# Turning attention probabilities by DMA instead of on TensorE, in a two-layer decoder trunk

## The chip, the cores and the metric

The kernel runs on one core of one Trainium2 chip. Its metric is the device time of one execution in microseconds (us). The core's engines work in parallel, each through its own queue in order, and wait for each other by semaphores: TensorE (PE) multiplies matrices, VectorE (DVE), ScalarE (ACT) and GpSimd (POOL) do elementwise work, SyncE (SP) issues the DMAs. In the profile PEld is PE's weight load.

## The reference, cut to what matters

A sequence of 256 tokens of width 1024 goes through two layers, each an attention mixer and a SwiGLU feed-forward block (FFN), and a last normalisation, all in float32.

```python
def dilated_mixer(h, w_in, w_out):            # layer 0, "mixer A": 16 heads of 64
    proj = (h @ w_in).reshape(B, S, N_GROUPS, 3, N_HEADS, HEAD_DIM)
    for g, (window, dil) in enumerate(((128, 1), (512, 4), (2048, 16))):
        q, k = partial_rotary(proj[:, :, g, 0], pos), partial_rotary(proj[:, :, g, 1], pos)
        o, lse = dilated_band_attention(q, k, proj[:, :, g, 2], dil, window // dil)
    wts = softmax(stack(lses))                # the three patterns are mixed by their denominators
    return einsum('gbsh,gbshd->bshd', wts, stack(outs)).reshape(B, S, ATTN_WIDTH) @ w_out

def forgetting_mixer(h, w_in, b_f, w_out):    # layer 1, "mixer B"
    s = einsum('bihd,bjhd->bhij', q, k) * scale + c[i] - c[j]   # c: running sum of log forget gates
    return einsum('bhij,bjhd->bihd', softmax(where(j <= i, s, NEG_INF)), v) @ w_out

for i in range(2):
    h = h + mixer[i](rmsnorm(h, norm[i]))
    h = h + (silu(gate) * up) @ w_down        # FFN on rmsnorm(h)
return rmsnorm(h, final_norm)
```

Scores come out with queries on partitions. To multiply the probabilities p with the values, PE needs the keys on partitions, so every 128x128 block of p has to be transposed in between.

## The kernel before, in words

**Matmuls.** Every float32 operand of a projection is split into a high and a low part, and `mm3` (L200 to L209) issues three matmuls for each product: high by high (L203), and the two mixed ones (L208). Weights come in pieces of 512 KB over SP's queue (L101, five buffers); ACT makes the high part (L80), DVE the low part (L84). The list `order` names the weights in the order of use; loads run two units ahead. Results are split in the same way: the attention output `ot` has a high part `oth` from ACT and a low part `otl` from DVE.

**Mixer A** works in four quarters (hq) of four heads, two head pairs (pr) each. The list `a_units` sets the units: per quarter six query and key units (w 0 and 1 of the three patterns g) and its value units (w 2). A unit is 48 matmuls of 256 columns; units that are written as a pair, like the dilated values of a quarter (patterns 1 and 2) or the undilated ones of quarters 0 and 1, are projected together, by `proj_pair`, 512 columns wide. The undilated values of quarters 2 and 3 are units by themselves (`proj_tok`). POOL copies the dilated values into place, 16 small copies a quarter (L285).

**Steps of attention** (`scores_0`, `scores_12`, `softmax_a`, the transposes, `pv_a`, the product with the values) are put between units: `later(i, step)` puts one behind unit i. Quarters 0 to 2 transpose by DMA (`turn_a`): POOL copies p so that the 16-bit halves of its numbers lie apart (L528), SP issues a DMA transpose of 10 blocks for each head (L530), ACT puts the halves together again (L531). Quarter 3 and all of mixer B transpose on PE, by multiplying with the identity into PSUM (`transposed`, L301), from where ACT or DVE copies (L306).

**out_proj** multiplies `ot` with the output weights: for each half t of the tokens 16 items of three 512-column matmuls, one for each n (half of the width) and k (128 rows of the weights; rows 2 hq and 2 hq + 1 belong to quarter hq). Attention steps that are still due are put between the items of the first half; the norm of that half's result (`norm_t`) lies between the last items of the second.

**Mixer B** has the same build in `b_units`: each quarter has a query, a key and a value unit. `scores_b` ends in a softmax on DVE (L906, L916) and ACT (L908, L915), with a bias that POOL masks (L880). In the program before, the transposes (`trans_b`) come one and a half units after the scores' unit and the product (`pv_b`, L313) two units after it, for all four quarters.

**What sets the order.** The scheduler keeps one queue per engine. It places instructions by the estimated time at which they can start; those under `first()` are put ahead of others. Once built, each engine's order is fixed.

## Time and profile before

| | us |
|---|---|
| median of 3 runs | 736.87 (736.38 to 737.0) |
| the profiled execution | 736.1 |
| its span, first to last instruction | 734.3 |
| PE busy | 726.4 |
| DVE, ACT, POOL busy | 495.9, 388.7, 83.0 |
| mean granted PE clock | 0.997 |

A row of groups has line, engine, operation, output <- inputs, size and count, then busy time, mean duration in ns, and the engine's idle time before it with its main releaser. A row of the timeline has start and duration in us first. A row of one line's view has minimum, median and maximum duration in ns, then the first and the last start.

### The profile page before, as it was taken

How to read it: one execution, taken by the hardware profiler on the slowest of the kernel's cores; microseconds unless marked ns; L12 is line 12 of the kernel's file. 1: busy time of each engine (PE TensorE's matmuls, PEld its weight loads, DVE VectorE, ACT ScalarE, POOL GpSimd, SP SyncE). 2: the span in 40 equal slices, each digit the busy share in tenths (PEclk: the TensorE clock that was granted, in tenths of full speed). 3: DMA queues.
4: the chain of work that ended last, by engine and by line, in shares of the span. 5: the costliest groups of instructions: out<-in, count | busy, mean ns of one | idle time of the engine just before them, and what ended most of it. 6: DMA issues, size and time to landing. Idle time of an engine off the chain costs nothing.

```text
span 734.3 us, 14310 instructions
## 1 busy us (share of the span) xinstructions
PE 726.4 (99%) x5856; PEld 672.4 (92%) x5856; DVE 495.9 (68%) x762; ACT 388.7 (53%) x617; POOL 83.0 (11%) x118
## 2 busy tenths in 40 slices
PE   9999999999999999999999999999999999999996
PEld 7999989999988899999999989999889999999995
DVE  6997998998996775554555474576776554556533
ACT  7646747738445663444554453587475444545421
POOL 0600206007105000000000004110010000000001
PEclk9999999999999999999999999999999999999998
DMA  9865955956864376656567352874547656656601
GB/s 335 306 202 174 237 182 153 289 193 152 268 194 160 116 241 221 195 179 203 195 202 247 127 168 90 294 260 138 172 142 237 222 179 203 195 188 218 198 1 58
DMA packets 55042, 141.93 MB, mean 193 GB/s; under 512 B 20257, under 2 KB 21441, under 8 KB 54977
## 3 DMA queue, kind: packets, MB, share of 16 engines
q1 hardware_dynamic: 54832, 140.88, 59.4%
q8 instruction: 46, 0.75, 0.4%
q14 instruction: 20, 0.16, 0.1%
q10 hardware_dynamic: 144, 0.15, 0.1%
HBM read 136.00 MB, written 1.07 MB: 187 GB/s over the span
## 4 chain that ended last, share of the span: by engine, by line
PE 97%; DVE 1%; ACT 1%; POOL 0%; issue 0%; POOLq 0%; DVEq 0%; ACTq 0%
PE ps_mm L208 34%; PE ps_mm L203 17%; PE ps_tr L208 9%; PE ps_sc L208 8%; PE ps_o L208 7%; PE ps_tr L203 5%; PE ps_sc L203 4%; PE ps_o L203 4%; PE ps_o L313 2%; PE ps_sc L395 2%; PE ps_tr L196 1%; PE ps_tr L301 1%; PE ps_sc L476 1%; PE ps_o L322 1%; PE ps_sc L894 0%; PE ps_sc L458 0%
## 5 line engine op out<-in xcount | busy, mean ns | idle before, releaser
L80 ACT ACTIVATE wh<-raw 128x1024 fp32r<-128x1024 f32 x236 | 243.4, 1054 | 207.1 <-PE ps_tr L208 66.7
L84 DVE TENSOR_TENSOR wl<-raw,wh 128x1024 fp32r<-128x1024 f32 x236 | 288.3, 1242 | 82.6 <-ACT wh L80 82.4
L203 PE MATMUL ps_mm<-xt,wh 128*128 128x256 f32 x816 | 227.2, 279 | 0.2 <-ACT v L281 0.2
L208 PE MATMUL ps_mm<-xt,wl 128*128 128x256 f32 x816 | 226.0, 277 | 0.0
L208 PE MATMUL ps_mm<-xt,wh 128*128 128x256 f32 x816 | 226.0, 277 | 0.0
L203 PEld LDWEIGHTS ps_mm<-xt,wh 128*128 128x128 f32 x816 | 153.1, 188 | 2.2 <-issue 1.7
L208 PEld LDWEIGHTS ps_mm<-xt,wl 128*128 128x128 f32 x816 | 153.6, 188 | 0.1
L208 PEld LDWEIGHTS ps_mm<-xt,wh 128*128 128x128 f32 x816 | 153.4, 188 | 0.0
L208 PE MATMUL ps_tr<-xt,wh 128*128 128x256 f32 x304 | 83.9, 276 | 0.0
L208 PE MATMUL ps_tr<-xt,wl 128*128 128x256 f32 x304 | 83.9, 276 | 0.0
L203 PE MATMUL ps_tr<-xt,wh 128*128 128x256 f32 x304 | 83.7, 276 | 0.0
L730 DVE TENSOR_TENSOR sa<-ps_tr,sa 128x256 f32<-128x256 f32 x38 | 16.1, 424 | 73.5 <-PE ps_tr L208 73.5
L208 PEld LDWEIGHTS ps_tr<-xt,wh 128*128 128x128 f32 x304 | 57.1, 188 | 0.0
L208 PEld LDWEIGHTS ps_tr<-xt,wl 128*128 128x128 f32 x304 | 57.0, 188 | 0.0
L203 PEld LDWEIGHTS ps_tr<-xt,wh 128*128 128x128 f32 x304 | 57.0, 188 | 0.0
L203 PE MATMUL ps_mm<-wh,xt 128*128 128x512 f32 (+1 forms) x144 | 49.8, 346 | 0.0
L173 POOL TENSOR_SCALAR rs<-ssq 128x1 f32<-128x1 f32 x7 | 1.9, 271 | 420.6 <-ACT junk L182 420.6
L208 PE MATMUL ps_mm<-wl,xt 128*128 128x512 f32 (+1 forms) x149 | 49.1, 335 | 0.0
L208 PE MATMUL ps_mm<-wh,xt 128*128 128x512 f32 (+1 forms) x149 | 49.1, 335 | 0.0
L285 POOL COPY v<-v 32x256 f32<-32x256 f32 x64 | 40.5, 632 | 71.2 <-ACT v L281 68.6
L203 PE MATMUL ps_sc<-wh,ah 128*128 128x512 f32 x80 | 31.4, 392 | 0.0
L208 PE MATMUL ps_sc<-wl,ah 128*128 128x512 f32 (+1 forms) x82 | 31.3, 385 | 0.0
(232 smaller groups left out, 1113.6 us busy)
## 6 DMA issues: line engine op xcount, KB each, us to landing
raw<-in_gu SPq DMA_DIRECT2D x88, 512.0 KB, 4.8
raw<-in_a_in SPq DMA_DIRECT2D x68, 512.0 KB, 5.0
raw<-in_dn SPq DMA_DIRECT2D x44, 512.0 KB, 4.7
raw<-in_b_in SPq DMA_DIRECT2D x24, 512.0 KB, 5.0
raw<-in_a_out SPq DMA_DIRECT2D x8, 512.0 KB, 5.0
raw<-in_b_out SPq DMA_DIRECT2D x8, 512.0 KB, 4.4
bias<-sums SPq DMA_DIRECT2D x8, 384.0 KB, 6.6
grow<-in_norms SPq DMA_DIRECT2D x4, 512.0 KB, 5.7
```

The source lines that it names most:

```text
L80: a = nc.scalar.activation(view(hi), src, AF.Copy)
L84: return nc.vector.tensor_tensor(view(lo), src, view(hi).bitcast(F32), op=ALU.subtract)
L196: nc.tensor.transpose(tr[:, k * P:(k + 1) * P], xn[:, kk * P:(kk + 1) * P], ident)
L203: nc.tensor.matmul(o, sh, mh, start=start, stop=False)
L208: last = nc.tensor.matmul(o[:, u], s, m[:, u], start=False, stop=end and u.stop == n)
L285: nc.gpsimd.tensor_copy(v[1 + a % 2][n:n + 32, a // 2 * S:a // 2 * S + S], by_t[a * 32:a * 32 + 32, t, g])
L301: nc.tensor.transpose(tr[:, i * P:(i + 1) * P], b, ident)
L313: nc.tensor.matmul(o[h * HD:(h + 1) * HD], v[:, c:c + HD], w(h), start=start, stop=stop)
L322: nc.tensor.matmul(o[:, :n], mhalf.to_broadcast([P, P]), mhalf.to_broadcast([P, n]), start=True, stop=True)
L395: nc.tensor.matmul(lead[t], xt[y][:, k, t * P:(t + 1) * P], w[z][:, u], start=k + y + z == 0, stop=k == KT - 1 and z == 1)
L476: nc.tensor.matmul(sc[h][c, o:o + 64], q[HR[h], pr, qb * P + a * 32:qb * P + a * 32 + 32], k[HR[h], pr].rearrange("p (b n) -> p b n", b=2) ...
L730: nc.vector.tensor_tensor(a, u, sg, op=ALU.mult)
```

## The change

Every probability block of both mixers is now transposed by DMA. `transposed`, `trans_a` and `trans_b` are gone. In mixer A quarter 3 turns through rooms of its own (`apart0`, `apart1`, and two tiles for what comes back) that serve both head pairs in turn, and the result is written over p. In mixer B `turn_b` does it for a pair of heads at once: the first pair's halves are put apart by POOL, the second's by DVE, one transpose of 12 blocks follows, and ACT puts the halves together in two copies.

The undilated values of quarters 2 and 3 become one pair, the last unit of mixer A; so pv_a of quarters 2 and 3 move into out_proj, which is rewritten: with `at=(4, 16)` they stand before item 4 and item 16, where four items of the second token half have been moved ahead. The norm lies over 8 items of the second half instead of 12. In mixer B, pv_b of quarters 0 and 1 keep their places (behind units 7 and 9), that of quarters 2 and 3 go into out_proj, and quarter 3's scores come half a unit earlier.

```diff
-        a_units += (..., v12, [(hq, 0, 2)] + v12, v12 + [(hq, 0, 2)])[hq]
+        a_units += (..., v12, v12, v12 + [(2, 0, 2), (3, 0, 2)])[hq]
...
     def turn_a(quad, pr):
...
+        last = quad["hq"] == 3
+        if last and pr == 0:
+            quad["room"] = [(hrow(f"apart{h}")[:, :640], p_tile(640)) for h in range(2)]
         for h in range(2):
...
+            with first():
+                apart, turned = quad["room"][h] if last else (home(("pt", "bias")[pr]), None)
+                w = p if last else apart
+                apart = apart.bitcast(U16)
+                nc.gpsimd.tensor_copy(apart.rearrange("p (t c) -> p t c", t=2), parted(p))
+                if not last:
+                    turned = home(("bias", "pt")[pr * (h == 0)])
+                turned = turned.bitcast(U16)
+                nc.sync.dma_start_transpose(turned.rearrange("p (g c) -> p g c", c=P), apart)
+                nc.scalar.copy(parted(w), turned.rearrange("p (t c) -> p t c", t=2))
...
                     for pr in range(2):
-                        if hq == 3:
-                            later(step(hq) + pr, trans_a, quad, pr)
-                        else:
-                            later(j + 1, turn_a, quad, pr)
+                        later(j + 1, turn_a, quad, pr)
                     for pr in range(2):
-                        later(step(hq) + 2, pv_a, quad, pr)
+                        later((15, 22, 40, 41)[hq], pv_a, quad, pr)
...
+        cols = lambda t, *ks: [(t, n, k) for i in ks for n in range(2) for k in (2 * i, 2 * i + 1)]
+        head = cols(0, 0, 1, 2) + cols(1, 0)[:early]
+        last = None
+        for i, item in enumerate(head + [None]):
+            if i in at:
                 with tc.issue_after(last.ins):
+                    for fn, a in due.pop(min(due)):
+                        fn(*a)
+            if item:
+                last = part(item)
+        last = part(*cols(0, 3))
+        res = [residual(accs[0], h[0], f"h_{nm}0")]
+        part(*cols(1, 0)[early:])
+        with tc.issue_after(last.ins):
+            part(*cols(1, 1, 2))
+            norm_t(*res[0], grow, xt, 0)
+            part(*cols(1, 3))
...
-    hs, xt = out_proj("a_out", ot, x, g_f, 6, 6, ("sc", "mm"))
+    hs, xt = out_proj("a_out", ot, x, g_f, (4, 16), 4, ("sc", "mm"))
...
+    def turn_b(hq, pr):
+        b = bq[hq]
+        w = b["w", pr] = b["bias", pr] if hq == 3 else turn_tile()
+        apart = w.bitcast(U16).rearrange("p (h t c) -> p h t c", h=2, t=2)
+        for h in range(2):
+            with first():
+                (nc.gpsimd, nc.vector)[pr].tensor_copy(apart[:, h], parted(b["pt"][pr, h][:, :3 * P]))
+        with first():
+            turned = ap.tile([P, D], F32, tag="xn", name="turned", bufs=2)[:, :6 * P].bitcast(U16)
+            nc.sync.dma_start_transpose(turned.rearrange("p (g c) -> p g c", c=P), w.bitcast(U16))
+            turned = turned.rearrange("p (h t c) -> p h t c", h=2, t=2)
+            for h in range(2):
+                nc.scalar.copy(parted(w[:, h * 3 * P:(h + 1) * 3 * P]), turned[:, h])
...
-                later(j, scores_b, hq)
+                later(j - (hq == 3) / 2, scores_b, hq)
+                for pr in range(2):
+                    later(j - (hq == 3) / 2, turn_b, hq, pr)
+                for pr in range(2):
+                    later((7, 9, 13, 14)[hq], pv_b, hq, pr)
...
-                later(j + 1.5, trans_b, hq)
-                for pr in range(2):
-                    later(j + 2, pv_b, hq, pr)
...
-    hs, xt = out_proj("b_out", ot, [h for h, _ in hs], g_f, 6, 9, ("mm", "sc"))
+    hs, xt = out_proj("b_out", ot, [h for h, _ in hs], g_f, (4, 16), 4, ("mm", "sc"))
```

The order of ACT at the end of mixer A, before: the last exponentials of quarter 3 (L289), weight splits, the copies of its undilated values (L263), the copies of PE's transposes (L306), and the splits of pv_a(3)'s two results.

```order
L289 ACTIVATE p,den<-p,nm 128x384
L80 ACTIVATE wh<-raw 128x1024 x2
L263 ACTIVATE v<-ps_mm,rs_a 128x256 x2
L80 ACTIVATE wh<-raw 128x1024 x2
L306 COPY pt<-ps_tr 128x512
L306 COPY pt<-ps_o 128x512
L306 COPY pt<-ps_tr 128x512
L306 COPY pt<-ps_o 128x512
L80 ACTIVATE oth<-ps_o 128x2x4x32 x2
```

The same place in the changed kernel (the exponentials are L285 there). L516 copies a turned head of quarter 3, L268 the paired values, two instructions for each token half.

```order
L285 ACTIVATE p,den<-p,nm 128x384
L80 ACTIVATE wh<-raw 128x1024 x2
L516 COPY p<-p 128x2x640 x2
L80 ACTIVATE wh<-raw 128x1024 x2
L268 ACTIVATE v<-ps_o,rs_a 128x256 x2
L516 COPY p<-p 128x2x640 x2
L268 ACTIVATE v<-ps_o,rs_a 128x256 x2
L80 ACTIVATE wh<-raw 128x1024 x2
L80 ACTIVATE oth<-ps_o 128x2x4x32 x2
L80 ACTIVATE wh<-raw 128x1024 x2
L80 ACTIVATE oth<-ps_o 128x2x4x32 x2
```

The values of the second token half now stand behind the turned copies of quarter 3's second head pair, and the results of pv_a(3) behind two weight splits.

POOL at that place, changed (before, the 16 value copies of quarter 3 stood there alone): value copies, here L281, and the putting apart of quarter 3's heads, L511.

```order
L281 COPY v<-v_2784 32x256 x8
L511 COPY apart_2730<-p 128x1280
L511 COPY apart_2732<-p 128x1280
L281 COPY v<-v_2784 32x256 x8
L511 COPY apart_2730<-p 128x1280
L511 COPY apart_2732<-p 128x1280
```

The first head pair's copies stand behind eight value copies, the second's behind all sixteen.

ACT at the output projection of mixer B, changed: L895 puts turned heads together, first quarter 2's four copies and later quarter 3's; between lie quarter 3's exponentials (L871) and scalings (L878), its values (L261), and the splits of pv_b(2)'s results.

```order
L895 COPY pt<-turned 128x2x384 x4
L871 ACTIVATE p,den_b<-p,nm_b 128x128
...
L871 ACTIVATE p,den_b<-p,nm_b 128x256
L80 ACTIVATE wh<-raw 128x1024
L80 ACTIVATE oth<-ps_o 128x256
L878 ACTIVATE p<-p,c_b 128x128 x2
L80 ACTIVATE oth<-ps_o 128x256
L80 ACTIVATE wh<-raw 128x1024
L895 COPY bias<-turned 128x2x384 x2
L80 ACTIVATE wh<-raw 128x1024
L895 COPY bias<-turned 128x2x384 x2
```

Quarter 3's softmax stands behind the copies that wait for quarter 2's transposes, and the result of pv_b(2) behind that softmax. On DVE the low parts of that result stand behind the putting apart of quarter 3's second head pair.

## The prediction

> **What bounds the kernel now.** I read the page's busy shares, then its slices and the chain that ended last, then the costliest group.

> ```profile
> PE 726.4 (99%) x5856; PEld 672.4 (92%) x5856; DVE 495.9 (68%) x762; ACT 388.7 (53%) x617; POOL 83.0 (11%) x118
> ...
> PE   9999999999999999999999999999999999999996
> ...
> PEclk9999999999999999999999999999999999999998
> ...
> PE 97%; DVE 1%; ACT 1%; POOL 0%; issue 0%; POOLq 0%; DVEq 0%; ACTq 0%
> ...
> L203 PE MATMUL ps_mm<-xt,wh 128*128 128x256 f32 x816 | 227.2, 279 | 0.2 <-ACT v L281 0.2
> ```

> TensorE (PE) is busy in every slice, at the full granted clock, and is 97% of the chain; its largest group idled 0.2 us in 816 matmuls. So there is no wait left to remove: a gain can only come from PE work removed, and every new wait of PE adds its full length. Both have to be priced in PE's own order of time.

> **What PE saves.** The columns of these rows are start, duration, engine and line.

> ```profile
> 225.75 0.40 PE L208 MATMUL ps_sc<-wl,oth 128*128 128x512 f32 x1
> ...
> 229.40 0.39 PE L208 MATMUL ps_sc<-wh,otl 128*128 128x512 f32 x1
> 229.63 0.81 PE L301 MATMUL ps_tr<-ident,p 128*128 128x128 f32 x6
> 230.29 0.60 PE L301 MATMUL ps_o<-ident,p 128*128 128x128 f32 x4
> 230.64 0.48 PE L203 MATMUL ps_sc<-wh,oth 128*128 128x512 f32 x1
> 230.96 0.40 PE L208 MATMUL ps_sc<-wl,oth 128*128 128x512 f32 x1
> ```
> ```profile
> 481.34 1.04 PE L301 MATMUL ps_tr<-ident,p 128*128 128x128 f32 x8
> 482.21 0.60 PE L301 MATMUL ps_o<-ident,p 128*128 128x128 f32 x4
> 482.57 0.37 PE L203 MATMUL ps_mm<-xt,wh 128*128 128x256 f32 x1
> 482.77 0.28 PE L208 MATMUL ps_mm<-xt,wh 128*128 128x256 f32 x1
> ```

> Durations overlap, so I price by starts. From 225.75 to 229.40 lie 16 steps of 512 columns: 0.228 us each. Ten transposes hold PE from 229.63 to 230.64, 1.01 us, and the next matmul takes 0.32 instead of 0.23 to its successor: 1.10 us a group. There are two such groups (quarter 3 of mixer A): 2.2 us. Twelve transposes take 481.34 to 482.57, 1.23, and 0.08 of restart, 1.31; four groups (mixer B): 5.3 us. The change removes all six, **7.5 us**, the only gain.

> [...]

> The paired projection saves nothing. The rows below are 256-wide steps.

> ```profile
> 170.71 0.28 PE L203 MATMUL ps_mm<-xt,wh 128*128 128x256 f32 x1
> ...
> 171.85 0.28 PE L208 MATMUL ps_mm<-xt,wh 128*128 128x256 f32 x1
> ```

> Ten steps in 1.14 us are 0.114 each; two value units are 96 × 0.114 = 10.9 us, a pair is 48 × 0.228 = 10.9. The reordered output projection issues the same matmuls.

> **What a turn by DMA costs, and where PE will wait.** Four views: the pieces of a turn before (POOL splits halves, SP issues the transpose, ACT copies back), its last instance in time, and mixer A's quarter 3.

> ```profile
> L528 POOL COPY pt<-p x12: 1247/1358/2245, 72.2 to 183.4; 128x1280 uint16<-128x1280 uint16 x12
> ```
> ```profile
> L531 ACT COPY pt<-turned x12: 1647/1672/1698, 77.5 to 188.5; 128x1280 uint16<-128x1280 uint16 x12
> ...
>   DMA turned<-pt: 14.5, 8
> ```
> ```profile
> 183.42 1.59 POOL L528 COPY pt<-p 128x1280 uint16<-128x1280 uint16 x1
> 185.04 1.36 SPq L530 DMA_TRANSPOSE turned<-pt  x1
> ```
> ```profile
> 188.49 1.67 ACT L531 COPY pt<-turned 128x1280 uint16<-128x1280 uint16 x1 [6.85 <-DMA turned<-pt]
> ```
> ```profile
> 213.06 1.48 PE L476 MATMUL ps_sc<-fm,fm 64*32 64x64 f32 x128
> 219.69 8.72 POOL L285 COPY v<-v 32x256 f32<-32x256 f32 x13 [33.33 <-ACT v L281]
> 221.89 1.74 DVE L508 TENSOR_SCALAR p<-p,c 128x256 f32<-128x256 f32 x4
> ```

> From the end of POOL's copy (185.01) to the start of ACT's (188.49) pass 3.48 us. ACT stood idle 14.5 us in all for such landings: whatever is queued behind a turn copy on ACT waits with it. PE did not wait for them, since the turned values were wanted more than a unit later.

> *Mixer A, quarter 3.* T0 is the end of its last scores, 214.54. The changed order of ACT puts the token-half copy of the paired values (L268, second pair of instructions) behind the turn copies of quarter 3's second head pair (L516), and pv_a(2) needs it. PE gets there after 24 + 48 + 12 steps of 512, 84 × 0.228 = 19.2, and two short products: T0 + 19.5. ACT gets there so. POOL starts the value copies at T0 + 5.15 and takes 8.72/13 = 0.67 each; eight end at T0 + 10.5 (the first pair's probabilities are there, 223.63 = T0 + 9.1). Two splits of 1.36: 13.2. Eight more value copies: 18.6. Two splits: 21.3. Landing: 24.8. Turn copy: 26.5. Value copy, 0.4 (half of the row below): 26.9. **PE waits 7.4 us.**

> ```profile
> 225.72 0.84 ACT L263 ACTIVATE v<-ps_mm,rs_a 128x256 f32<-128x256 f32 x2 [0.35 <-PE ps_mm L208]
> ...
> 226.45 2.01 ACT L80 ACTIVATE wh<-raw 128x1024 fp32r<-128x1024 f32 x2
> ```

> Bounds: value copies at their median and splits at 1.25 give 3 us, value copies at 0.74 (an estimate: the row's 0.67 and a tenth) and splits at 1.59 give 10.

> ```profile
> L285 POOL COPY v<-v x64: 392/402/1467, 25.2 to 231.1; 32x256 f32<-32x256 f32 x64
> ```

> After pv_a(3) the split of its result stands on ACT behind two weight splits (2.01 us above) and PE goes straight to items that need it, after 2.4 us of products: 0.7 (0 to 1.4).

> *Mixer B, quarter 0.* PE returns for pv_b two units after the scores, as before, but now the turn lies between.

> ```profile
> 472.00 0.82 PE L894 MATMUL ps_tr<-fb,fb 64*128 64x128 f32 x8
> ```
> ```profile
> 479.80 0.68 ACT L915 ACTIVATE p<-p,c_b 128x128 f32<-128x128 f32 x2
> ...
> 481.34 0.68 ACT L915 ACTIVATE p<-p,c_b 128x128 f32<-128x128 f32 x2
> ```

> Scores end at S0 = 472.82; the head pairs are ready at 480.48 and 482.02, S0 + 7.7 and + 9.2. A copy of 768 halves is not in the trace; scaled from 1280 it is 0.82 on POOL and 1.0 on ACT, and on DVE I take POOL's (0.4 to 1.3). First pair: 7.7 + 1.65 + 3.48 + 2.0 = 14.8. Second: landed at 9.2 + 1.6 + 3.48 = 14.3, copied behind the first's, 16.8. PE comes at 96 steps of 0.117 (481.10 to 481.34 below has two) = 11.2: it idles 3.6, does the first product in 0.7, idles 1.3: **4.8 us** (3.5 to 7).

> ```profile
> 481.10 0.28 PE L208 MATMUL ps_mm<-xt,wh 128*128 128x256 f32 x1
> ```

> *Quarter 1.* Scores end at S1 = 488.51; no table load, so the pairs are ready at 493.01 and 494.44, S1 + 4.5 and + 5.9.

> ```profile
> 487.69 0.82 PE L894 MATMUL ps_tr<-fb,fb 64*128 64x128 f32 x8
> ```
> ```profile
> 492.40 0.61 DVE L916 TENSOR_SCALAR p<-p,c_b 128x256 f32<-128x256 f32 x2
> ```
> ```profile
> 489.29 0.40 ACT L908 ACTIVATE p<-p,nm_b 128x128 f32<-128x128 f32 x1 [0.67 <-DVE nm_b L906]
> ...
> 493.75 0.69 ACT L915 ACTIVATE p<-p,c_b 128x128 f32<-128x128 f32 x2 [0.24 <-DVE c_b L913]
> ```

> Ready in ACT at 11.6 and 13.6 against 11.2: 0.4 + 1.3 = **1.7 us** (0 to 4).

> *Quarters 2 and 3.* pv_b(2) sits four items into b_out and is ready in time, just (S3 + 5.4 against 5.5 below). But on ACT quarter 3's exponentials stand behind quarter 2's four turn copies. Those end, by the same sums and one weight split on DVE between, at S2 + 15.3; scores_b(3) end at S3 = S2 + 72 × 0.117 + 1.5 = S2 + 9.9. So ACT starts the softmax at S3 + 5.4, takes 5.15 for it (489.29 to 494.44), and 2.3 for a value copy, a weight split and a result split between: S3 + 12.9. DVE's two splits for quarter 3 wait for that (1.6) and stand ahead of the result's low part: 15.1 with it. PE asks for it at S3 + 2.8 + 2.7 + 1.4 + 2.7 + 0.5 = 10.1. **5.0 us** (0.5 to 7). After pv_b(3) weight splits precede the result split as in A, on both engines: 1.3 (0 to 2.5).

> Costed at nothing: quarter 2 of A turns two units ahead of its use; the norm inside a_out is covered by 8 items instead of 12, 5.5 us instead of 8.2, under which PE did not wait: at most the 2.7 of difference; weights behind a waiting ACT stand a unit or two (5.5 us each) ahead, and gain time while PE waits; with that cover gone each costs what a turn copy waits, up to 3.5. ACT's and DVE's dropped PSUM copies were off the path.

> **Sum.** −7.5 + 7.4 + 0.7 + 4.8 + 1.7 + 5.0 + 1.3 = +13.4 on the profiled execution's 736.1 us (span 734.3, 1.8 around it): 749.5. The median of the runs is 736.87, 0.8 above that execution: **750.3 us**. Lower bounds: −7.5 + 3 + 3.5 + 0.5 = −0.5; upper: −7.5 + 10 + 1.4 + 7 + 4 + 7 + 2.5 = +24.4, 736.4 to 761.3.

> **Rivals.** *All of it hidden*: 736.87 − 7.5 = 729.4, faster. The mechanism is one: the turned copies are back before PE asks, which decides from a chain 7.4 us shorter in A and 5 in B. For it: every earlier turn cost PE nothing, and the landing is only 3.5 us. Against: the splits and ACT copies alone, with no landing at all, already pass S0 + 11.2 in quarter 0.
> *One attention stalls, the other not*: B hidden gives −7.5 + 8.1 = +0.6, 737.5; A hidden gives −7.5 + 12.8 = +5.3, 742.2. For it: the ACT position of one copy decides A, and POOL's copies have a median of 0.40 us.
> *A slow restart*: after a long idle stretch PE may run at half speed for a while. The start of the span shows it.

> ```profile
> 4.93 1.85 PE L395 MATMUL ps_sc<-wh,xt 128*128 128x512 f32 x4
> 6.62 0.62 PE L395 MATMUL ps_sc<-wl,xt 128*128 128x512 f32 x2
> 7.08 1.08 PE L395 MATMUL ps_sc<-wh,xt 128*128 128x512 f32 x4
> ```

> Four matmuls of 512 take 1.69 us there, 0.42 each, and 0.23 from 7.08 on. At least 0.8 us was lost; if the first 5.7 us of PE's work ran so, 2.6. With three idle stretches above 3.5 us (A, quarter 0, b_out) that is 2.3 to 7.9 more: 755. Against: the granted clock reads 9 in that slice too.
> [...]
> *Not done as said*: PE's changed order holds no transpose of probabilities, so this has no weight.

> **Chances.** Stalls as summed 0.60 (742 to 757 by itself), slow restart on top 0.14, one attention alone 0.17, all hidden 0.09. The range of 738 to 762 leaves out the hidden case and the lowest of the third. A difference under 0.2% (1.5 us) can't be told from none: faster 0.10, within it 0.06 (B hidden), slower 0.84.

> **What would show it.** Right: PE idle of 5 to 9 us in the first product of pv_a(2), released by ACT's value copy, ACT idle before L516 for the DMA; 4 to 6 us before pv_b(0), released by L895; and one in b_out released by DVE's low part. Granted clock below 9 in those slices would speak for the restart. Wrong: PE still 99% busy with a span near 727, or DMA transposes landing in well under 3 us, or value copies on POOL at 0.4 us throughout.

## The result and the profile after

The changed kernel takes 760.67 us (median of four runs, 754.36 to 761.67) against 736.93 for the kernel before on the same chip: ratio 1.030, interval 1.0245 to 1.036. The forecast was 750.3 with 738 to 762: the sign and the range held, the time itself is 10 us higher, nearer to the rival "slow restart on top" (755) than to the sum. The profiled execution has a span of 758.2 us, 23.9 more than before.

The page of the changed kernel: PE's busy row, the slices of PE and of its granted clock, the chain that ended last by engine.

```profile
PE 733.6 (97%) x5742; PEld 669.7 (88%) x5742; DVE 499.1 (66%) x756; ACT 407.6 (54%) x633; POOL 93.5 (12%) x130
...
PE   9999999999996999999999999989899999999996
...
PEclk9999999999997999999999999979999999999998
...
PE 56%; ACT 3%; DMA 3%; DVE 2%; issue 1%; SPq 0%; POOL 0%; POOLq 0%; DVEq 0%; ACTq 0%
```

PE has 114 instructions fewer and is busy 7.2 us longer (726.4 before). Three slices show a hole (6, 8 and 8 instead of 9), and in two of them the granted clock is 7 instead of 9. The chain now leaves PE for ACT and DMA. PE's waits in the changed kernel: engine, line, what it waited for, us in total, times, the longest.

```profile
PE ps_o L295 <- ACT v L268: 5.5, 1, 5.5
PE ps_o L295 <- ACT pt L895: 4.8, 3, 3.1
PE ps_mm L203 <- ACT v L261: 3.4, 1, 3.4
PE ps_o L295 <- issue: 1.5, 1, 1.5
...
PE ps_mm L203 <- DVE qk L425: 0.6, 1, 0.6
PE ps_sc L203 <- ACT oth L80: 0.3, 1, 0.3
```

Three places carry it. **The end of mixer A**, PE's and then ACT's timeline (start, duration, instruction, and in brackets the idle time before it with its releaser):

```profile
230.47 0.65 PE L295 MATMUL ps_o<-pt,v 128*64 128x256 f32 x4 [1.51 <-issue]
236.64 3.68 PE L295 MATMUL ps_o<-pt,v 128*64 128x128 f32 x44 [5.52 <-ACT v L268]
```
```profile
229.54 0.83 ACT L268 ACTIVATE v<-ps_o,rs_a 128x256 f32<-128x256 f32 x2
232.50 1.61 ACT L516 COPY p<-p 128x1280 uint16<-128x1280 uint16 x1 [2.12 <-DMA p<-apart]
234.65 1.61 ACT L516 COPY p<-p 128x1280 uint16<-128x1280 uint16 x1 [0.55 <-DMA p<-apart]
236.13 0.82 ACT L268 ACTIVATE v<-ps_o,rs_a 128x256 f32<-128x256 f32 x2
```

PE stands 1.5 and 5.5 us at pv_a(2). What ends the long wait is one copy of 0.4 us, the values of the second token half, which stands on ACT behind two turned heads that wait for their transposes. The page names no releaser for the short wait ("issue"), but PE goes on at 230.47, just after the copies of the first token half (229.54 to 230.37).

**Quarter 0 of mixer B**, PE and ACT:

```profile
498.40 2.44 PE L295 MATMUL ps_o<-pt,v 128*64 128x256 f32 x8 [3.05 <-ACT pt L895]
500.78 0.79 PE L857 MATMUL ps_sc<-fb,fb 64*128 64x128 f32 x2
```
```profile
497.31 3.83 ACT L895 COPY pt<-turned 128x768 uint16<-128x768 uint16 x4 [2.10 <-DMA turned<-pt]
```

**The output projection of mixer B**, PE and ACT:

```profile
542.27 0.80 PE L203 MATMUL ps_mm<-wh,oth 128*128 128x512 f32 x1 [3.41 <-ACT v L261]
```
```profile
536.74 2.89 ACT L895 COPY pt<-turned 128x768 uint16<-128x768 uint16 x3 [0.63 <-DMA turned<-pt]
...
541.64 0.57 ACT L261 ACTIVATE v<-ps_mm 128x512 f32<-128x512 f32 x1
```

After each of the three, the clock is low. Windows of 3.41 us of the changed kernel (window, its length, busy us and instructions of PE, PEld, DVE, ACT, POOL, then the granted clock, DMA share, GB/s):

```profile
228.22:231.64 3.42, 1.39 (x8) 0.51 (x6) 2.91 (x2) 2.15 (x4) 2.96 (x2) 1.00 0.45 86
231.64:235.05 3.41, 0.00 (x0) 0.00 (x0) 0.62 (x1) 2.01 (x2) 0.00 (x0) 0.50 0.86 164
235.05:238.46 3.41, 1.82 (x24) 1.63 (x26) 0.53 (x1) 3.41 (x5) 0.00 (x0) 0.50 0.98 335
238.46:241.88 3.42, 3.42 (x28) 2.83 (x25) 2.98 (x4) 1.55 (x3) 0.00 (x0) 0.50 0.58 196
241.88:245.29 3.41, 3.41 (x17) 2.80 (x16) 0.00 (x0) 0.00 (x0) 0.00 (x0) 1.00 0.50 179
...
494.46:497.88 3.42, 0.89 (x8) 0.69 (x6) 3.14 (x4) 1.31 (x2) 0.00 (x0) 1.00 1.06 170
497.88:501.29 3.41, 2.89 (x10) 1.54 (x10) 0.00 (x0) 3.41 (x6) 0.00 (x0) 0.50 0.96 276
501.29:504.70 3.41, 3.41 (x12) 1.54 (x10) 0.42 (x1) 0.57 (x2) 0.00 (x0) 0.50 0.58 228
504.70:508.12 3.42, 3.42 (x17) 2.56 (x17) 2.03 (x14) 2.84 (x9) 0.00 (x0) 0.50 0.00 0
508.12:511.53 3.41, 3.41 (x32) 3.41 (x31) 2.88 (x12) 3.41 (x13) 1.20 (x2) 1.00 0.70 208
...
538.84:542.25 3.41, 0.02 (x1) 0.00 (x0) 0.79 (x3) 3.41 (x13) 0.00 (x0) 1.00 0.76 264
542.25:545.66 3.41, 3.39 (x10) 2.16 (x12) 1.30 (x4) 2.87 (x9) 1.60 (x2) 0.50 0.07 17
```

Half clock holds from 231.64 to 241.88, from 497.88 to 508.12 and from 542.25 to 545.66. PE worked 5.2, 9.7 and 3.4 us in them (1.82 + 3.42; 2.89 + 3.41 + 3.42; 3.39). A matmul of 512 columns takes 0.427 us from its start to the next there, 0.227 elsewhere in this trace, so at full clock this work would take little more than half: up to **9.2 us** lost, an estimate by halving.

The account of the 23.9 us from the page: PE's idle time is 758.2 − 733.6 = 24.6 against 734.3 − 726.4 = 7.9, **+16.7**; half clock **+9.2**; so the rest of PE's busy time fell by 2.0 only (7.2 − 9.2), not by the 7.5 of the removed transposes. A matmul's row of 512 columns lasts 0.39 us in this trace, and its successor starts 0.23 after it, so each wait shows 0.16 us too short and the shortest not at all. PE's starts close the account. I took each matmul's time from its own start to the next one's, less the idle time between, and compared it with the mean of its kind in the kernel before. The work that was removed is 7.1 us. The matmuls that start at half clock take 10.6 us longer, with what short waits lie between them. The others take 3.7 us longer, of which 2.6 lie in mixer A, mostly in its projections, and 1.0 in quarter 1 of mixer B. The sum is −7.1 + 16.7 + 10.6 + 3.7 = +23.9.

### The profile page after: what moved, and what is told of

It is laid out like the page before. It is cut to its first block, busy times and chain, and to the rows that moved or that the text cites. A ratio compares the mean times of both kernels' runs of the same rounds, so it can differ in the third digit from the quotient of the medians.

```text
span 758.2 us, 14166 instructions
## 1 busy us (share of the span) xinstructions
PE 733.6 (97%) x5742; PEld 669.7 (88%) x5742; DVE 499.1 (66%) x756; ACT 407.6 (54%) x633; POOL 93.5 (12%) x130
## 4 chain that ended last, share of the span: by engine, by line
PE 56%; ACT 3%; DMA 3%; DVE 2%; issue 1%; SPq 0%; POOL 0%; POOLq 0%; DVEq 0%; ACTq 0%
PE ps_mm L208 13%; PE ps_tr L208 9%; PE ps_sc L208 7%; PE ps_mm L203 7%; PE ps_o L208 6%; PE ps_tr L203 5%; PE ps_sc L203 3%; PE ps_o L203 3%; DMA turned<-pt 2%; ACT p L871 1%; DMA raw<-in_b_in 1%; PE ps_o L295 1%; DVE wl L84 1%; ACT pt L895 1%; PE ps_tr L196 1%
## 5 line engine op out<-in xcount | busy, mean ns | idle before, releaser
L80 ACT ACTIVATE wh<-raw 128x1024 fp32r<-128x1024 f32 x236 | 243.9, 1055 | 214.2 <-PE ps_tr L208 67.6
L84 DVE TENSOR_TENSOR wl<-raw,wh 128x1024 fp32r<-128x1024 f32 x236 | 291.3, 1252 | 101.6 <-ACT wh L80 101.2
L203 PE MATMUL ps_mm<-xt,wh 128*128 128x256 f32 x816 | 227.7, 279 | 0.7 <-DVE qk L425 0.6
L208 PE MATMUL ps_mm<-xt,wl 128*128 128x256 f32 x816 | 226.6, 278 | 0.1
L208 PE MATMUL ps_mm<-xt,wh 128*128 128x256 f32 x816 | 226.4, 278 | 0.0
L203 PEld LDWEIGHTS ps_mm<-xt,wh 128*128 128x128 f32 x816 | 153.6, 188 | 3.1 <-issue 2.4
L208 PEld LDWEIGHTS ps_mm<-xt,wl 128*128 128x128 f32 x816 | 154.0, 189 | 0.5 <-DVE wl L84 0.5
L208 PEld LDWEIGHTS ps_mm<-xt,wh 128*128 128x128 f32 x816 | 153.6, 188 | 0.0
L208 PE MATMUL ps_tr<-xt,wl 128*128 128x256 f32 x304 | 83.9, 276 | 0.0
L208 PE MATMUL ps_tr<-xt,wh 128*128 128x256 f32 x304 | 83.9, 276 | 0.0
L203 PE MATMUL ps_tr<-xt,wh 128*128 128x256 f32 x304 | 83.7, 276 | 0.0
L208 PEld LDWEIGHTS ps_tr<-xt,wl 128*128 128x128 f32 x304 | 57.1, 188 | 0.0
L208 PEld LDWEIGHTS ps_tr<-xt,wh 128*128 128x128 f32 x304 | 57.1, 188 | 0.0
L203 PEld LDWEIGHTS ps_tr<-xt,wh 128*128 128x128 f32 x304 | 56.9, 188 | 0.0
L281 POOL COPY v<-v 32x256 f32<-32x256 f32 x64 | 34.6, 540 | 111.1 <-ACT v L277 108.5
L203 PE MATMUL ps_mm<-wh,xt 128*128 128x512 f32 (+1 forms) x112 | 41.0, 366 | 0.1
L208 PE MATMUL ps_mm<-wl,xt 128*128 128x512 f32 (+1 forms) x117 | 40.3, 352 | 0.0
L208 PE MATMUL ps_mm<-wh,xt 128*128 128x512 f32 (+1 forms) x117 | 40.3, 351 | 0.0
L203 PE MATMUL ps_sc<-wh,ah 128*128 128x512 f32 x80 | 31.4, 392 | 0.0
L208 PE MATMUL ps_sc<-wl,ah 128*128 128x512 f32 (+1 forms) x82 | 31.3, 385 | 0.0
```

Source lines behind the costliest of these rows:

```text
L80: a = nc.scalar.activation(view(hi), src, AF.Copy)
L84: return nc.vector.tensor_tensor(view(lo), src, view(hi).bitcast(F32), op=ALU.subtract)
L203: nc.tensor.matmul(o, sh, mh, start=start, stop=False)
L208: last = nc.tensor.matmul(o[:, u], s, m[:, u], start=False, stop=end and u.stop == n)
L281: nc.gpsimd.tensor_copy(v[1 + a % 2][n:n + 32, a // 2 * S:a // 2 * S + S], by_t[a * 32:a * 32 + 32, t, g])
```

## The experiments

**Theories.** W: the time is the waits that the prediction names, nothing else (743 for either attention alone). R: waits plus half clock after them. The experiments ask which attention pays what, whether the named queue positions cause the waits, and what sets the clock.

| kernel | median us | ratio to before | interval |
|---|---|---|---|
| A changed alone | 746.64 | 1.0136 | 1.0116 to 1.0156 |
| B changed alone | 748.86 | 1.0178 | 1.0154 to 1.0202 |
| A's copies behind the values | 756.45 | 1.0273 | 1.0252 to 1.0293 |
| A's copies behind the results too | 752.04 | 1.0223 | 1.0199 to 1.0248 |
| pv_b(0), pv_b(1) a unit later | 757.66 | 1.0298 | 1.0279 to 1.0317 |
| last values of B copied by DVE | 760.37 | 1.0339 | 1.0320 to 1.0357 |
| unread matmuls at two waits | 757.23 | 1.0285 | 1.0258 to 1.0312 |
| unread matmuls at all waits | 762.93 | 1.0355 | 1.0334 to 1.0376 |
| all repairs together | 745.93 | 1.0137 | 1.0121 to 1.0154 |
| A alone, repaired | 736.62 | 1.0003 | 0.9993 to 1.0013 |

### One attention at a time

A alone keeps mixer B, its transposes and its output projection as before; B alone keeps mixer A so.

```diff
# A alone: the program before, in mixer B
-                for pr in range(2):
-                    later(j - (hq == 3) / 2, turn_b, hq, pr)
+                later(j + 1.5, trans_b, hq)
...
# B alone: the program before, in mixer A
-        a_units += (..., v12, v12, v12 + [(2, 0, 2), (3, 0, 2)])[hq]
+        a_units += (..., v12, [(hq, 0, 2)] + v12, v12 + [(hq, 0, 2)])[hq]
```

> Mixer A as changed, mixer B and its output projection as before. Waits and half clock: the first half of the changed kernel's trace is 11.1 us longer than before up to the second norm of FFN 0, so about 748 us, with one stretch of half clock behind pv_a(2). Waits alone (the low clock has nothing to do with them): -2.2 for two transpose groups, +7.6 of idle time, +0.7 for one wait in an early unit: about 743. If something that both parts share costs the time, neither part alone shows its share, and this stays under 741.

> Mixer B and b_out as changed, mixer A as before. Waits and half clock: the rest of the 23.9 us of span, 12.8, so about 750 us, with half clock behind the waits at pv_b(0) and in b_out and none in mixer A. Waits alone: -5.3 for four groups, +8.2 of idle time, +2.9 for products of pv_b(0) that no longer run in pairs: about 743.

Measured +10.5 and +12.7 us over 736.17, together 23.2: the two costs add up, and W's 743 is too low for both. Half clock: 6.83 us in A alone (233.93 to 240.76), 10.24 and 3.41 in B alone. For A alone it is not the whole of what W lacks: PE worked only 2.7 us in that stretch, 1.4 lost by halving, and short waits for DVE and ACT in earlier units are 3.5 us in this trace, where the expectation has 0.7.

### Mixer A's end: the order of ACT

First the turned copies of quarter 3's second head pair are held behind the paired values.

```diff
-                nc.scalar.copy(parted(w), turned.rearrange("p (t c) -> p t c", t=2))
+                back = (parted(w), turned.rearrange("p (t c) -> p t c", t=2))
+                if last and pr:
+                    held_back.append(back)
+                else:
+                    nc.scalar.copy(*back)
...
-                    v_pair(vs, lead[t], t, r_a[t])
+                    copied = v_pair(vs, lead[t], t, r_a[t])
+                for back in held_back:
+                    with first(), tc.issue_after(copied.ins):
+                        nc.scalar.copy(*back)
```

> The changed kernel, but ACT puts quarter 3's second head pair together only after it has copied the paired values; PE's, POOL's and SP's orders are the same. If the place on ACT is what pv_a(2) waits for: its wait of 7.0 us falls to about 1 and the half clock behind it goes too (2.6 us): 752 us. If only the wait counts and the low clock comes by itself: 754 to 755, with half clock still there. If POOL and the transposes set the time, whoever stands first on ACT: no change, 760.

The wait for the values is gone, and 2 to 4 us with it, not the 8.7 expected. PE's and ACT's timeline of this kernel:

```profile
237.70 0.50 PE L203 MATMUL ps_sc<-wh,oth 128*128 128x512 f32 x1 [1.92 <-ACT oth L80]
```
```profile
232.42 1.64 ACT L619 COPY p<-p 128x1280 uint16<-128x1280 uint16 x1 [1.41 <-DMA p<-apart]
```

The copies, still waiting for their transposes, now stand ahead of the splits of pv_a(2)'s results, and PE waits for those. So I held them behind these splits as well.

```diff
-        split(ot, lambda x: x[:, kt, :].rearrange("p (b u a) -> p b a u", a=4, b=2), src)
+        cut, _ = split(ot, lambda x: x[:, kt, :].rearrange("p (b u a) -> p b a u", a=4, b=2), src)
+        if quad["hq"] == 2 and pr == 1:
+            for back in held_back:
+                with first(), tc.issue_after(cut.ins):
+                    nc.scalar.copy(*back)
```

> The changed kernel, but ACT puts quarter 3's second head pair together only after it has split both results of pv_a(2). With only the paired values put ahead, the wait moved: the results of pv_a(2) then stood behind those turned copies (2.2 us on ACT's and 0.8 on DVE's part) and half clock stayed for 3.4 us. If those copies' place on ACT is the whole cause in mixer A: all but 1.5 us of the waits there and the half clock go, about 751 us. If quarter 3's turn is late for pv_a(3) as well: the wait moves on to pv_a(3), and the time stays at 755 to 757.

752.04: of A's waits at its end only 1.5 us (released by "issue") and the two of about 0.3 stay, and no window there is at half clock. From the start to mixer B's first scores it takes 474.4 us instead of 482.3 (471.2 before the change). The queue position on ACT is the cause of A's wait of 5.5 us.

### Mixer B: three places

One unit of room more for pv_b of quarters 0 and 1:

```diff
-                    later((7, 9, 13, 14)[hq], pv_b, hq, pr)
+                    later((8, 10, 13, 14)[hq], pv_b, hq, pr)
```

> The changed kernel with pv_b of quarters 0 and 1 one unit later (5.6 us). If the turn's length against two units of cover is the cause: their waits (3.05 and 1.7 us) go, and with them the 10.2 us of half clock and the broken pairs of products behind pv_b(0), 3 to 6 more: 750 to 753 us. If quarters 0 and 1 hand their delay on (tiles for turned probabilities are three, and free up one unit later): new waits at quarters 1 and 2, 757 or above.

757.66, by its time the second branch. Quarter 0's wait and its half clock are gone, and quarter 1's wait stays (1.4 us, 1.5 in the changed kernel); and PE waits further on, at the scores of quarter 3, here PE's and ACT's timeline:

```profile
529.07 1.22 PE L857 MATMUL ps_sc<-fb,fb 64*128 64x128 f32 x6 [3.97 <-ACT fb L953]
```
```profile
519.21 1.95 ACT L895 COPY pt<-turned 128x768 uint16<-128x768 uint16 x2 [3.18 <-DMA turned<-pt]
```

ACT idles 3.18 us ahead of a turned copy; the later exponentials, and behind them the copy of quarter 3's features (L953), are late by it. This points to the order of ACT's whole queue in mixer B, more than to one deadline of PE; no run isolates it.

The last values of B copied by DVE instead of ACT, so that output projection needn't wait for ACT's exponentials to get its PSUM bank:

```diff
-            bq[hq][w] = v_tile(o)
+            v = bq[hq][w] = v_tile()
+            with first():
+                nc.vector.tensor_copy(v, o)
```

> The changed kernel with the last values of mixer B copied by DVE instead of ACT, where they stood behind quarter 3's exponentials and kept the PSUM bank that b_out's second accumulator needs. If that bank alone costs: its 3.4 us and 1.4 of half clock go: 756. If, as forecast, the low part of pv_b(2)'s result is as late: the wait comes back at items k = 4 and 5, and the time stays at 759 to 761.

The bank wait fell from 3.4 to 1.6 us, and the wait for the low part that the prediction expects there did not appear. The time did not move (760.37): in the profiled execution half clock is gone from b_out, but the wait at quarter 1 is 2.4 us instead of 1.5, with two windows at half clock behind it (519.53 to 526.36). So this run shows who holds the bank, not what it costs.

All repairs together; besides the three, B's turned copies of quarters 2 and 3 are held behind quarter 3's softmax and pv_b(2)'s splits, and `out_proj` has six early items and its attention steps ahead of items 10 and 16:

```diff
-                nc.scalar.copy(parted(w[:, h * 3 * P:(h + 1) * 3 * P]), turned[:, h])
+                back = (parted(w[:, h * 3 * P:(h + 1) * 3 * P]), turned[:, h])
+                if hq >= 2:
+                    (held_back if hq == 2 else held_b).append(back)
+                else:
+                    nc.scalar.copy(*back)
...
-        head = cols(0, 0, 1, 2) + cols(1, 0)[:early]
+        ahead = cols(1, 0, 1)
+        head = cols(0, 0, 1) + ahead[:early] + cols(0, 2)
...
+    hs, xt = out_proj("a_out", ot, x, g_f, (10, 16), 6, ("sc", "mm"))
```

> All of it together: the turned copies of the late quarters held on ACT behind what PE needs first (values, exponentials, result splits), pv_b of quarters 0 and 1 one unit later, the last values by DVE, and out_proj with six items of the second token half ahead of k = 4 and 5, products at items 10 and 16. If waits and the half clock that they cause are the whole of the loss, what is left is the saved PE time: 736.2 - 7.5 = 728.7, with 1 to 3 us of small waits 730 to 732, below both kernels. If the transposes cost something that no place hides (traffic that delays weights, splits on POOL that slow DVE): 735 or above.

745.93, where 730 to 732 was expected: still 10 us slower than before. Its waits of PE:

```profile
PE ps_sc L868 <- ACT fb L976: 2.4, 1, 2.4
PE ps_o L295 <- ACT pt L914: 1.9, 2, 1.7
PE ps_mm L203 <- DVE v L997: 1.9, 1, 1.9
```

Mixer A's end is clean; in B the waits moved and shrank, and each of three still puts one window of 3.41 us at half clock. Since A could be repaired and B not, I took A by itself (A alone, with the held copies and the new order of `out_proj`):

> Mixer A alone changed, mixer B as before, with the turned copies held on ACT behind pv_a(2)'s result splits and the new out_proj's products at items 10 and 16: no wait of PE is left at the end of mixer A. If those waits were all: the two saved transpose groups show, 736 - 2.2 = 734. If the turn costs in other places too (splits and copies that stand before what PE needs in earlier units: waits of 0.6 and 1.1 us were seen there): 735.5 to 738.

736.62, the same as before within 0.13% either way. What A saves on PE (2.2 us) is eaten by small waits for DVE in the query and key units of earlier quarters, which the kernel before does not have and whose cause stays open:

```profile
PE ps_mm L203 <- DVE fm L439: 1.6, 2, 1.0
PE ps_mm L203 <- DVE qk L439: 0.6, 1, 0.6
```

No version was faster than the kernel before.

### The clock

Matmuls whose result nobody reads, put in so that PE is busy while it would wait: 56 ahead of pv_a(2), 24 ahead of pv_b(0).

```diff
+    def warm(x, n):
+        o = psum("o")
+        for _ in range(n):
+            nc.tensor.matmul(o[:, :S], x[0][:, 0, :P], x[0][:, 0, :S], start=True, stop=True)
...
+        if quad["hq"] == 2 and pr == 0:
+            warm(xt, 56)
...
+        if (hq, pr) == (0, 0):
+            warm(xt, 24)
```

> The changed kernel, with matmuls that nobody reads on PE just ahead of pv_a(2) (56 of 256 columns, 6.4 us) and of pv_b(0) (24, 2.7 us): less than the waits there, so the waits end when they did, but PE is busy in them. Half clock from idle time: no half clock at these two places, about 2.6 us less behind pv_a(2) and 3.4 to 6 less behind pv_b(0): 752 to 755 us; b_out keeps its own. If the clock falls for another reason (the transposes' traffic, the small products), it falls here too and the time stays at 760 or above.

The windows of this kernel at the two places, and at the third, which was left alone:

```profile
229.74:233.16 3.42, 3.42 (x31) 3.42 (x30) 1.27 (x1) 1.66 (x1) 0.19 (x1) 1.00 0.85 155
495.99:499.41 3.42, 2.85 (x16) 1.23 (x16) 0.00 (x0) 3.42 (x5) 0.00 (x0) 1.00 0.91 305
533.53:536.95 3.42, 0.00 (x0) 0.00 (x0) 0.79 (x3) 3.42 (x16) 1.11 (x2) 1.00 0.31 121
536.95:540.36 3.41, 3.33 (x8) 2.12 (x10) 2.32 (x5) 3.38 (x9) 0.48 (x1) 0.50 0.55 104
```

With PE kept busy (3.42 and 2.85 of 3.42 us) the granted clock stays at 1.00 at the first two places; at the third PE is busy 0.00, and the window behind reads 0.50. So in this kernel idle time is the cause of the low clock. The price is less sure. From T0, the end of mixer A's last scores, to mixer B's first scores it takes 271.5 us instead of 272.8, and from the start of quarter 0's scores to the end of quarter 1's 21.2 instead of 25.0: 5.0 us less, where halving gives 2.6 + 4.9 = 7.5 for these two places. The profiled span is 5.3 us shorter than the changed kernel's (752.9), but the mean of the runs, relative to the kernel before, only by 0.17%, 1.3 us, with intervals that overlap.

The trace also tells what the short wait ahead of pv_a(2) is:

```profile
PE ps_o L522 <- ACT v L268: 1.4, 1, 1.4
```

The unread matmuls (L522) use no values, and still wait 1.4 us for the value copy L268. The paired values are summed in the PSUM banks (`lead`, tag `o`) that pv_a(2) writes next, and ACT has not emptied the first of them. The product also reads these values, but the bank alone holds PE as long.

Filling all the waits in the same way failed as a measurement:

```diff
+            if nm == "b_out" and i == 2:
+                with tc.issue_after(last.ins):
+                    last = warm(ot, 26)
```

> The changed kernel with unread matmuls ahead of all of PE's long waits: pv_a(2) (56 of 256 columns), the products of quarters 0 (24 and 8) and 1 (6 and 10) of mixer B, and b_out's third item (26). Each set is shorter than its wait, so the waits keep their ends. If the clock falls only because PE idles: no half clock before the end of the program, and what is left is the price of the waits alone, 760.7 less half of the 5.2 + 9.7 + 3.4 us of work at half clock, 751 to 752 us. If the half clock comes without idle time, or the matmuls push the waits on: 755 or above.

762.93, no faster than the change itself (the intervals overlap). The matmuls in b_out only moved the wait for the bank behind them (2.3 us stay), so their time was added to it. Between 541.06 and 544.47 lies the only half clock of this kernel before its end. But the 130 unread matmuls, at 0.114 us or more from start to start, are at least 14.8 us, and 9.5 us of waits stay: 24.3 against 17.3 of waits in the changed kernel. They lasted longer than the waits that they were to fill, so this time says nothing on the price of the clock.

Then the clock by itself, in the kernel before, by waits of PE for a chain of n small ACT copies in the feed-forward block. First six of growing length:

```diff
+        def gap(n, last):
+            tr = psum("tr")
+            a, b = (ap.tile([P, D], F32, tag="xn", name="gap", bufs=2) for _ in range(2))
+            with tc.issue_after(last.ins):
+                nc.tensor.matmul(tr[:, :P], ident, ident, start=True, stop=True)
+            with first():
+                nc.scalar.activation(a[:, :P], tr[:, :P], AF.Copy)
+                for i in range(n):
+                    nc.scalar.activation((b, a)[i % 2][:, :P], (a, b)[i % 2][:, :P], AF.Copy)
+            return tc.issue_after(nc.tensor.matmul(tr[:, P:2 * P], ident, (a, b)[n % 2][:, :P], start=True, stop=True).ins)
...
+                n = {5: 10, 9: 13, 11: 16, 13: 19, 15: 22, 17: 26}.get(f, 0) if l == 0 else 0
+                with gap(n, last) if n else nullcontext():
+                    last = up(f)
```

> The kernel before, with six waits of growing length put into FFN 0, where PE is otherwise dense: ahead of units 5, 9, 11, 13, 15 and 17 PE waits for a chain of 11 to 27 small copies on ACT (about 0.3 us each, of which some 3 us lie beside matmuls). If idle time has to fill a whole window of 3.4 us: half clock only behind waits of 3.4 us and more. If a window with much idle time is enough: half clock already from about 2 us on, depending on where the wait falls in the window. In both cases it lasts a multiple of 3.4 us. If the clock has nothing to do with waits: none.

No half clock after 2.60 us of idle; 6.83 us of it after 3.6, 4.6 and 5.6; 10.24 after the two longest (10.4 and 8.0). That looked like a bound on length between 2.6 and 3.6. But with the copies held behind the values, above, 1.92 and 0.54 us of idle had been enough, and the changes of the clock lie a multiple of 3.41 us apart (6.83 and 10.24 here; in the changed kernel 231.64 and 542.25 are 91 times 3.413 apart). So the last run put in eight waits of about 2.3 and eight of about 1.6 us:

```diff
+                n = (9, 7)[l] if f % 2 and 5 <= f <= 19 else 0
```

> The kernel before with sixteen waits of TensorE put into the two feed-forward blocks, one ahead of every second unit, each a chain of small ScalarE copies: eight of about 2.3 us in the first block, eight of about 1.6 us in the second (from the earlier run: ten links gave 2.60 us idle, 0.33 us for each link more; here nine and seven). Theory formed from the runs so far: the clock is set for windows of 3.41 us on a fixed grid, and a window in which TensorE was busy for less than about 0.47 of the time is followed by one at half clock. By it a wait of 1.6 us never halves the clock (a window keeps at least 0.53), and one of 2.3 us does where at least 1.8 us of it falls into one window: (3.41 - 2.3 + 2 x 0.5) / 3.41 = 0.6 of the positions, so about 5 of the 8 (3 to 7), and which ones can be read from the busy share of the window: every window below 0.45 followed by half clock, none above 0.53, stretches of 3.41 us or a multiple. Rival, the length of the idle stretch alone decides, with its bound between 2.6 (no half clock in the earlier run) and 3.05 us (half clock in the changed kernel): no half clock at any of the sixteen. Second rival, any wait over about 1.5 us halves the clock by chance or load: some of the second block's too. The time itself: 736 + 8 x 2.3 + 8 x 1.6 + about 1.2 us for each half stretch = 767 without, 773 with five.

Six of the first eight came out as one stretch of 2.21 to 2.26 us, the others as 5.0 and 1.0. Two equal ones, PE's timeline:

```profile
319.38 0.56 PE L743 MATMUL ps_tr<-gap,ident 128*128 128x128 f32 x2 [2.21 <-ACT gap L742]
361.16 0.49 PE L743 MATMUL ps_tr<-gap,ident 128*128 128x128 f32 x2 [2.21 <-ACT gap L742]
```

and the windows of the clock around them:

```profile
316.25:319.66 3.41, 1.20 (x8) 0.70 (x6) 1.44 (x2) 2.83 (x10) 0.00 (x0) 1.00 0.83 251
319.66:323.08 3.42, 3.42 (x18) 3.42 (x18) 0.00 (x0) 0.00 (x0) 0.00 (x0) 0.50 0.67 232
323.08:326.49 3.41, 3.41 (x32) 3.41 (x31) 0.00 (x0) 0.39 (x1) 0.00 (x0) 1.00 0.01 5
357.21:360.62 3.41, 1.74 (x8) 1.11 (x6) 2.25 (x2) 3.19 (x10) 0.00 (x0) 1.00 0.90 275
360.62:364.03 3.41, 2.87 (x25) 2.87 (x26) 0.00 (x0) 0.46 (x2) 0.00 (x0) 1.00 0.80 294
```

The first lies inside one window, which has PE busy 1.20 of 3.41 us: the next is at half clock. The second, just as long, lies across two (1.74 and 2.87): the granted clock stays at 1.00. Of the six, four halved the clock; none of the 1.5 us waits did. Length alone, and chance, are both out. The time, 790.78, was missed by 18 us (773 expected): a wait costs more around it than its idle time, which this run does not divide further.

## Why the prediction was right and where it was wrong

**What bounds the kernel, and what PE saves.** Right that there was no wait to remove; idle time of PE is the largest part of the loss. The saving of 7.5 us was right too: by PE's starts it is 7.1.

**Where the miss of 10 us lies.** The profiled spans, cut at mixer B's scores, against the terms of the forecast:

| stretch | forecast, us | measured, us |
|---|---|---|
| up to quarter 0's scores | −2.2 + 7.4 + 0.7 = +5.9 | +11.0 |
| from there to the end of quarter 1's scores | −1.3 + 4.8 = +3.5 | +7.7 |
| to the end of quarter 2's scores | −1.3 + 1.7 = +0.4 | +1.9 |
| the rest, with b_out | −2.6 + 5.0 + 1.3 = +3.7 | +3.2 |

Mixer A lost 5.1 us more than forecast: 2.5 are matmuls at half clock, 2.6 are matmuls, mostly of its projections, that follow each other a little more slowly. The forecast has no term for the latter; their cause stays open. Quarter 0 lost 4.2 more, in its stretch at half clock. Quarter 1 lost 1.5 more, 1.0 of it in products that follow each other more slowly.

**Mixer A, quarter 3, 7.4 us**: 1.51 + 5.52 = 7.0, at the named product. The 5.52 lie behind the named copy and are gone when its place is changed; the 1.51 stay, a wait for a PSUM bank that the prediction does not have. The tail after pv_a(3), 0.7: 0.3 from ACT and 0.3 from DVE.

**Quarters 0 and 1 of mixer B, 4.8 and 1.7 us.** Quarter 1 idles 1.48 + 0.26. In quarter 0 3.05 us show as idle, and the second pair's wait lies in a stretch at half clock where waits and slow products can't be told apart; with the unread matmuls, without half clock, it takes 21.2 us from the start of quarter 0's scores to the end of quarter 1's, 17.3 before, 1.3 of transposes saved: 5.3.

**b_out, 5.0 us for the low part of pv_b(2): this step failed.** The amount was near (3.4 idle and 1.7 of half clock), the cause was another. ACT starts quarter 3's exponentials at 539.50, 5.1 us after the scores (5.4 forecast); but PE was stopped earlier than at the product that needs the low part. The second accumulator of the item list takes the PSUM bank of B's last value unit, and the copy that frees it (L261) stands among those exponentials. I had followed the operands of PE's next matmuls and not the banks that they write.

**Slow restart, priced as a rival at 0.14: the largest part of the miss.** The six terms of waits sum to 20.9 us in the forecast; measured are 16.7 of idle time, and some more that shows as slow steps. To that comes half clock, 9.2 us by halving; the unread matmuls gave back 5.0 of 7.5 at two of the places, so 9.2 is an upper estimate. The mechanism stood in the text with 2.3 to 7.9 us for three waits; it should have been a term of the sum, since the kernel's own first microseconds showed it (0.42 us a matmul of 512 columns, then 0.23) and three waits above 3.5 us were forecast. What I held against it was the digit 9 of the clock's first slice, but the trace's record of the clock begins only at 6.39 us, so that digit told nothing of the time before. In the changed kernel's trace half clock follows the window from 538.84 to 542.25, which has PE busy 0.02 of 3.41 us, but windows with more work did the same: 0.89 us from 494.46, 1.39 from 228.22, and in all repairs together 1.49 from 507.85. By halving, the three stalls cost 2.6, 4.9 and 1.7 us here, and the one in A alone 1.4. The stretch at half clock was longer than one window, 10.24 us, where its windows were partly idle (PE busy 0.00 and 1.82 us from 231.64) or held the narrow products of attention (2.89 and 3.41 from 497.88).

**Durations taken from afar**: 768 halves on DVE took 0.65 (0.8 taken), on ACT 1.05 (1.0), on POOL 0.83 (0.82); the landing in B was 3.7 to 4.9 us (3.48 taken), so quarter 0's first copy came later than forecast. The chain through POOL in mixer A, in its timeline of the changed kernel:

```profile
216.21 3.47 POOL L281 COPY v<-v 32x256 f32<-32x256 f32 x8 [33.53 <-ACT v L277]
219.74 2.56 POOL L511 COPY apart<-p 128x1280 uint16<-128x1280 uint16 x2
222.36 5.32 POOL L281 COPY v<-v 32x256 f32<-32x256 f32 x8
227.74 3.44 POOL L511 COPY apart<-p 128x1280 uint16<-128x1280 uint16 x2
```

Quarter 3's last scores end at T0 = 209.49 here. POOL starts at T0 + 6.7 instead of 5.15, but its first eight copies take 0.43 us each instead of 0.67: two errors that cancel. The second eight take 0.67, the last split ends at 231.18 = T0 + 21.7 (21.3 forecast), the last landing takes 3.47 (to 234.65; 3.48 taken), and PE goes on at 236.64 = T0 + 27.1 (26.9 forecast), having come at T0 + 19.5 as forecast.

**Rivals.** "All of it hidden" and "one attention alone" are out by the runs of each attention: both stall. **What would show it**: at pv_a(2) the idle time (7.0, of which L268 released 5.5) and ACT's idle time before L516 came as named, and so did the clock below 9, the sign of the restart. L895 released pv_b(0), but after 3.05 us that show, not 4 to 6. The low part in b_out did not come. Of the signs of being wrong, value copies at 0.4 us came for the first eight only.

## What to carry to other kernels

In these kernels ACT works through its queue in order, and a copy that waits for a DMA delays all that stands behind it: a value copy of 0.4 us behind two turned heads kept PE waiting 5.52 us. Before work is moved off the bounding engine to a DMA round trip (3.4 to 5.2 us from issue to landing in the changed kernel), look at what its return copy will stand in front of, and which operands *and PSUM banks* hang on that. Holding the return copies back repaired mixer A, but only to a tie; in mixer B the wait moved from place to place. A wait of TensorE that left a window of the clock little busy (0.02 to 1.39 of 3.41 us in the changed kernel) cost more than its length: 1.7 to 4.9 us more a stall there and 1.4 in A alone, estimated as half of what PE worked at half clock.
